# Roots of the input by groups in the first stage and another order of the last tiles, in a hybrid retention and attention step on one core

## The chip, the core and the metric

The kernel runs on one core of one Trainium2 chip. A core has five engines that run side by side, each through its own queue of instructions in order: PE (matrix products; its weight loads are listed apart as PEld), DVE (vectors), ACT (scalar functions and copies), POOL (GpSimd) and SP (here it only issues DMAs). Products are summed in PSUM banks; everything else lives in SBUF, which DMAs fill from the main memory. The metric is the device time of one execution in microseconds (us), the median of several runs.

## The reference, cut to what matters

The kernel computes one layer of a diffusion backbone for 128 context tokens and 512 latent tokens, all of width 1024, in float32. The change touches the two ends of the layer: the first modulated RMSNorm with what it feeds, and the last RMSNorm.

```python
def rms_scale(x):
    xf = x.astype(jnp.float32)
    return xf * lax.rsqrt(jnp.mean(xf * xf, axis=-1, keepdims=True) + EPS)

def adaln(cond, w_mod, b_mod):
    m = jax.nn.silu(cond) @ w_mod + b_mod
    return jnp.split(m[..., None, :], 6, axis=-1)

...
sh1, sc1, g1, sh2, sc2, g2 = adaln(c, w_mod[l], b_mod[l])
h = rmsnorm(xs, norm1_g[l]) * (1.0 + sc1) + sh1      # start: norm and modulation
y, _ = token_mixer(h, *mix_w, pos_lat, ctx)          # its first product is h @ w_in
...
xs = xs + g2 * conv_ffn(h, w_up[l], conv_w[l], conv_b[l], w_down[l])
y_sample = rmsnorm(xs, final_g)                      # end: last norm
```

## The kernel before

The 640 tokens are five tiles of 128: tile 0 is the context, tiles 1 to 4 the latent tokens. A float32 product is made of three products of rounded parts: each operand is split into a high part (a rounded copy) and a low part (the rest), and `mm3` (lines 158 to 161) multiplies high by high, high by low and low by high.

**The order of the work.** A planner of the programming layer gives each engine its order from the dependencies and its own estimate of times. Inside a `manual_schedule` block the engines that it names keep the order in which the program writes their instructions, and only work of other parts of the program may be put between. In the first stage (from line 406) these are PE, DVE and ACT; in the last (from line 1481) DVE and PE, so ACT, POOL and SP are ordered by the planner there. Every engine waits for the data of its next instruction and holds back what stands behind it.

**The first stage, lines 289 to 467.** SP issues all loads at the start, in a fixed order (lines 98 to 106 and 326 to 336): constants and small vectors, the five token tiles, and then by turns pieces of the adaLN weights `w_mod` (`mod_load`; five groups that serve 1, 1, 2, 2 and 2 of the eight column blocks k of the activations) and of the key and value weights (`kv_load`). The order of these loads is: mod 0, kv 0 and 1, mod 1, kv 2 and 3, mod 2, kv 4 to 7, mod 3, mod 4, the rest of the constants. None of them reuses a buffer.

- `x_square(t)` squares a token tile on ACT and sums it up, which takes an activation and the readout of its accumulator. `x_scale` takes the root of the sums by an integer estimate and three Newton steps on DVE (`rsqrt`, lines 202 to 220) for three tiles, later for two, and multiplies the tiles by it (line 349). `x_trans(t)` turns a tile over by eight PE transposes into two PSUM banks (line 356; there are five banks) and copies them out (line 358) to `xnT`, on ACT or DVE.
- `mod_mm(g)` (line 368) multiplies the condition by one group of `w_mod`, `mod_row` (line 376) copies the result out, and `mod_vec` (line 382) turns it into a vector by two small PE products, which DVE finishes (lines 384 and 386).
- `mod_hi(k)` scales and shifts block k on DVE (line 391) and makes its high part on ACT (line 393); `mod_lo(k)` makes the low part on DVE (line 396). `kv_hi` (line 319, ACT) and `kv_lo` (line 324, DVE) split the key and value weights in the same way, two blocks at a time.
- `z_kv(k)` multiplies block k of all five tiles by block k of these weights, 15 products of 512 columns into five banks that are summed over the eight blocks. Its argument `mid` puts a `mod_vec` between its second and third token tile.

The next stage's weights go through two buffers (`w_raw`, line 136, and `w_split`, lines 147 and 152), so their loads wait until `kv_lo` has read the old contents.

**The last stage, lines 1467 to 1513.** The last down-projection adds into `x1`. `last(t, c0, n)` makes the products of n columns of tile t, `down_add` multiplies them by the gate and adds them to `x1` on DVE (lines 1224 and 1225), and `square` sums the squares on ACT (line 1242) into `s7`. Tile 4 is done in one half of 512 and two quarters of 256 columns. `root_sum` adds up the sums on DVE, takes the power -0.5 on POOL (line 1252) and `root` makes one Newton step on DVE (lines 1260 to 1264), first for tiles 0 to 2 together, and then for tile 3 and tile 4. `gain` multiplies half a tile by the final gain `fg` (line 1270, on POOL or DVE), and `out` multiplies it by the root, on ACT (line 1277), or, where `fused`, by root and gain in one step on DVE (line 1275), and issues its DMA on SP (line 1279). There are ten such outputs of 256 KB.

Of the kernel before, what the change touches and what calls it, by code (L numbers as in the profile page):

```python
# [12 lines left out]
AF = mybir.ActivationFunctionType  # L13
ALU = mybir.AluOpType
# [4 lines left out]
P = 128  # L19
DM = 1024  # L20
KD = DM // P
NT = 5
# [4 lines left out]
NF = FF // P  # L27
EPS = 1e-6
O_Q, O_K, O_RQ, O_RK, O_RV, O_RG, O_GA, O_GR = 0, 1024, 1536, 2048, 2560, 3584, 4608, 5632
C_ID, C_SEL, C_SEL1, C_JV, C_RF, C_RB, C_MF, C_MB, C_IQ, C_NH, C_W = 0, 128, 136, 140, 142, 270, 398, 526, 654, 786, 787  # L30
HW = 322


# [36 lines left out]
def hybrid_step(ctx: ExitStack, tc: tile.TileContext, a: dict, o: dict):  # L70
# [131 lines left out]
    def rsqrt(pool, ss, n, inv_n, post=1.0):  # L202
        m = pool([P, n], tag=f"nm{n}", bufs=2)
        it = pool([P, n], I32, tag=f"ni{n}", bufs=2)
        y = pool([P, n], tag=f"ny{n}", bufs=2)
        tt = pool([P, n], tag=f"nt{n}", bufs=2)
        V.tensor_scalar(m, ss, inv_n, EPS, op0=ALU.mult, op1=ALU.add)
        V.tensor_scalar(it, m.bitcast(I32), 1, None, op0=ALU.logical_shift_right)
        V.tensor_scalar(y.bitcast(I32), it, -1, 0x5F3759DF, op0=ALU.mult, op1=ALU.add)
        V.tensor_scalar(m, m, -0.5, None, op0=ALU.mult)  # L210
        for _ in range(3):
            if n == 1:
                V.scalar_tensor_tensor(tt, y, m, y, op0=ALU.mult, op1=ALU.mult)
            else:
                V.tensor_mul(tt, y, y)
                V.tensor_mul(tt, tt, m)
            V.scalar_tensor_tensor(y, tt, 1.5, y, op0=ALU.add, op1=ALU.mult)  # L217
        if post != 1.0:
            V.tensor_scalar(y, y, post, None, op0=ALU.mult)  # L219
        return y  # L220
# [95 lines left out]
    def kv_hi(k0):  # L316
        h, kk = k0 // 4, k0 % 4
        wkv[k0] = [wraw[h][:, kk * 512:(kk + 2) * 512]] + [wp([P, 1024], F32R, tag="wh", bufs=8) for _ in range(2)]
        nc.scalar.copy(wkv[k0][1], wkv[k0][0])

    def kv_lo(k0, *part):
        raw, hi, lo = wkv[k0]
        s = slice(512 * part[0], 512 * part[0] + 512) if part else slice(0, 1024)
        V.tensor_sub(lo[:, s], raw[:, s], hi[:, s].bitcast(F32))
# [14 lines left out]
        sq = hflat[1][:, :DM]  # L339
        nc.scalar.activation(sq, xin[:, t, :], AF.Square, accum_out=ss[:, t:t + 1])  # L340

    def x_scale(t0, t1_, on_act=()):
        rs = rsqrt(t1, ss[:, t0:t1_], t1_ - t0, 1.0 / DM)
        for t in range(t0, t1_):
            r = rs[:, t - t0:t - t0 + 1]
            if t in on_act:
                nc.scalar.activation(xin[:, t, :], xin[:, t, :], AF.Copy, scale=r)
            else:
                V.tensor_scalar(xin[:, t, :], xin[:, t, :], r, None, op0=ALU.mult)  # L349

    def x_trans(t):
        for g in range(2):
            ps = mm([P, 512], tag="mm")
            for j in range(4):
                k = g * 4 + j
                nc.tensor.transpose(ps[:, j * P:(j + 1) * P], xin[:, t, k * P:(k + 1) * P], ident)  # L356
            copy = V.tensor_copy if g and t > 1 else nc.scalar.copy
            copy(xnT[g][:, :, t * P:(t + 1) * P], ps.rearrange("p (k t) -> p k t", k=4))

    mrow, psm = {}, {}  # L360

    def mod_mm(g, row=True):
        m = MG[g][1]
        psm[g] = aux([P, 512], tag="aux")
        for i in range(KD * m // 2):
            for j in range(4):
                k, cc = (i, j % 2) if m == 2 else (2 * i + j % 2, 0)
                nc.tensor.matmul(psm[g][32 * j:32 * j + 32, :P], s128[:, k, :],
                                 wmod[g][:, j // 2, k, cc * P:(cc + 1) * P],
                                 start=i == 0, stop=i == KD * m // 2 - 1)  # L370
        if row:
            mod_row(g)

    def mod_row(g):
        mrow[g] = t1([P, P], tag="mrow", bufs=2)
        V.tensor_copy(mrow[g], psm[g][:, :P])

    def mod_vec(g):
        k0, n = MG[g]
        sel = C_SEL if n == 2 else C_SEL1  # L380
        ps = aux([P, 512], tag="aux")
        nc.tensor.matmul(ps[:, :4 * n], mrow[g], cst[:, sel:sel + 4 * n], start=True, stop=True)
        m = mvec[:, :, k0:k0 + n, :]
        V.tensor_add(m, ps[:, :4 * n].rearrange("p (v j c) -> p v j c", v=2, j=n),
                     cv[:, 4:6, k0:k0 + n].unsqueeze(3).to_broadcast([P, 2, n, 2]))
        V.tensor_mul(m[:, 0], m[:, 0], cv[:, 2, k0:k0 + n].unsqueeze(2).to_broadcast([P, n, 2]))

    def mod_hi(k):
        xk = xnT[k // 4][:, k % 4]
        for c, s in ((0, slice(P, TOK)), (1, slice(0, P))):  # L390
            V.tensor_scalar(xk[:, s], xk[:, s], mvec[:, 0, k, c:c + 1],  # L391
                            mvec[:, 1, k, c:c + 1], op0=ALU.mult, op1=ALU.add)
        nc.scalar.copy(hT[0][:, k, :], xk)  # L393

    def mod_lo(k):
        V.tensor_sub(hT[1][:, k, :], xnT[k // 4][:, k % 4], hT[0][:, k, :].bitcast(F32))

    def z_kv(k, mid=None):
        wh, wl = (x[:, (k % 2) * 512:(k % 2) * 512 + 512] for x in wkv[k - k % 2][1:])
        for t in range(NT):  # L400
            ts = slice(t * P, (t + 1) * P)
            mm3(kvb[t], hT[0][:, k, ts], hT[1][:, k, ts], wh, wl, k == 0, k == KD - 1)
            if mid is not None and t == 1:
                mod_vec(mid)

    with tc.manual_schedule(engines={ET.PE, ET.DVE, ET.Activation}):
        ps = aux([P, 512], tag="aux")
        nc.tensor.transpose(ps[:, :80], crow, ident[:80, :80])
        s128 = cond_tile(t1)
        V.tensor_copy(cv.rearrange("p i k -> p (i k)"), ps[:, :80])  # L410
        th = t1([P, 2, 8], tag="th0")
        nc.scalar.activation(th, cv[:, 0:2, :], AF.Tanh, scale=0.5)
        V.tensor_scalar(cv[:, 4, :], cv[:, 4, :], 1.0, None, op0=ALU.add)
        V.scalar_tensor_tensor(th, th, 1.0, cv[:, 0:2, :], op0=ALU.add, op1=ALU.mult)
        V.tensor_scalar(s32, th.rearrange("p c k -> p k c"), 0.5, None, op0=ALU.mult)
        V.tensor_copy(s128[:, :, 0:2], s32)
        for t in range(NT):
            x_square(t)
        x_scale(0, 3)
        x_trans(0)  # L420
        x_trans(1)
        kv_hi(0)
        x_scale(3, 5)
        x_trans(2)
        x_trans(3)
        x_trans(4)
        mod_mm(0)
        mod_vec(0)
        mod_mm(1, False)
        mod_hi(0)  # L430
        kv_lo(0, 0)
        mod_lo(0)
        mod_row(1)
        mod_vec(1)
        mod_hi(1)
        kv_lo(0, 1)
        mod_lo(1)
        kvb = [mm([P, 512], tag="mm") for _ in range(NT)]
        z_kv(0)
        kv_hi(2)  # L440
        kv_lo(2)
        mod_mm(2)
        z_kv(1, 2)
        mod_hi(2)
        mod_hi(3)
        mod_lo(2)
        mod_lo(3)
        z_kv(2)
        kv_hi(4)
        kv_lo(4)  # L450
        mod_mm(3)
        z_kv(3, 3)
        mod_hi(4)
        mod_hi(5)
        mod_lo(4)
        mod_lo(5)
        kv_hi(6)
        kv_lo(6)
        mod_mm(4)
        z_kv(4, 4)  # L460
        mod_hi(6)
        mod_hi(7)
        mod_lo(6)
        mod_lo(7)
        z_kv(5)
        z_kv(6)
        z_kv(7)
# [800 lines left out]
    def gain(t, c0, eng):  # L1268
        x = x1[:, t, c0:c0 + 512]
        eng.tensor_mul(x, x, fg[:, c0:c0 + 512])  # L1270
# [210 lines left out]
    with tc.manual_schedule(engines={ET.DVE, ET.PE}):  # L1481
        def last(t, c0, n):
            last_mm(t, c0, n, (2, 3) if t < NT - 1 else (0, 1, 2, 3))
            down_add(bank[t, c0], t, c0)
            square(t, c0, n)

        for t in range(3):
            last(t, 0, 512)
            gain(t, 0, nc.gpsimd)
            last(t, 512, 512)  # L1490
        last(3, 0, 512)
        root_sum(0, 3)
        gain(3, 0, nc.gpsimd)
        last(3, 512, 512)
        root(0, 3)
        for u in range(3):
            out(u, 0)
        for u in range(2):
            out(u, 512, True)
        gain(3, 512, nc.gpsimd)  # L1500
        root_sum(3, 1)
        last(4, 0, 512)
        root(3, 1)
        out(2, 512, True)
        out(3, 0)
        out(3, 512)
        last(4, 512, 256)
        last(4, 768, 256)
        gain(4, 0, V)
        root_sum(4, 1)  # L1510
        root(4, 1)
        out(4, 0)
        out(4, 512, True)
    t7.close()
# [36 lines left out]
```

## Time and profile before

| what | value |
|---|---|
| three runs | 1188.34, 1190.0 and 1190.55 us, median 1190.0 |
| the profiled execution | 1187.15 us, of which the profile's span is 1185.4 us |
| granted clock of PE, mean | 0.996 |
| DMA bytes in the span | 139.02 MB |

The profile lists, in us from the start of its span, what each engine ran: start, duration, engine, line, operation, the tile written and the tiles read with their shapes, and in brackets how long the engine was idle before and what ended that time. "PEq" or "SPq" is an engine's sequencer. Merged rows end in the number of instructions. The chain of waits goes back from the last instruction, at each step to what released it. The waits view lists who waited for whom: total, number of times, longest. The windows view gives, for chosen stretches, the length and then the busy time and number of instructions of PE, PEld, DVE, ACT and POOL, PE's granted clock, the busy share of the 16 DMA engines and GB/s. The DMA view counts the packets of a stretch by size; one line of it gives a queue's packets, MB and the share of the DMA engines' time that its packets took.

### The profile page before, as it was taken

What the parts mean: (1) busy time and instruction counts of PE and PEld (TensorE: products, weight loads), DVE (VectorE), ACT (ScalarE), POOL (GpSimd) and SP (SyncE); (2) the same over time, 40 slices, a digit from 0 to 9 for tenths busy, and PEclk for the clock granted to TensorE, in tenths of its full rate; (3) what the DMA queues carried; (4) which work ended last, traced back from release to release, by engine and by line L of the source; (5) the groups of instructions that cost most, each with busy time, mean ns of one, the idle gap of its engine ahead of it and who ended that gap; (6) DMA issues with size and microseconds to landing.
All of it is one profiled execution on the core that took longest, in us unless ns stands there. A gap on an engine that the chain in (4) does not pass through costs nothing.

```text
span 1185.4 us, 18331 instructions
## 1 busy us (share of the span) xinstructions
PE 1152.0 (97%) x7317; PEld 1038.4 (88%) x7317; DVE 740.2 (62%) x1431; ACT 567.9 (48%) x1020; POOL 172.3 (15%) x174
## 2 busy tenths in 40 slices
PE   4999999999999999999999999999999999999995
PEld 3788899999988888888999988999989999899994
DVE  5676977663234436463333349959767688588887
ACT  4355656551132324443222235558557466565464
POOL 0032200000012100033011122011112111121013
PEclk9999999999999999999999999999999999999998
DMA  8922111115554431112122539445666667566552
GB/s 282 301 94 72 37 36 36 36 48 169 212 191 172 147 98 45 36 37 71 36 72 72 192 109 163 113 93 103 149 132 134 142 138 164 125 120 152 130 123 108
DMA packets 130917, 139.02 MB, mean 117 GB/s; under 512 B 26240, under 2 KB 98000, under 8 KB 130832
## 3 DMA queue, kind: packets, MB, share of 16 engines
q1 hardware_dynamic: 106592, 112.95, 29.5%
q0 software_dynamic: 24240, 24.91, 13.8%
q8 instruction: 57, 0.93, 0.3%
q14 instruction: 28, 0.23, 0.1%
HBM read 110.32 MB, written 6.03 MB: 98 GB/s over the span
## 4 chain that ended last, share of the span: by engine, by line
PE 90%; DVE 5%; issue 1%; ACT 1%; POOL 1%; DMA 0%; SPq 0%; POOLq 0%; ACTq 0%; DVEq 0%
DMA xin.u1.1_112<-in_x_sample 0%; POOL f0.s.5_3525 L902 0%; DVE acts.u2.2_101 L1066 0%; DVE x1.u1.1_6381 L1225 0%; DVE x1.u1.1_6381 L1038 0%; DVE acts.u1.1_100 L1065 0%; PE mm7.mm.9_7501 L1348 0%; PE mm7.mm.45_9655 L1345 0%; PE mm7.mm.33_8923 L1345 0%; PE mm7.mm.57_10407 L1345 0%; PE mm7.mm.21_8191 L1345 0%; PE mm7.mm.18_7942 L1345 0%; PE mm7.mm.30_8674 L1345 0%; PE mm7.mm.42_9406 L1348 0%; PE mm7.mm.42_9406 L1345 0%
## 5 line engine op out<-in xcount | busy, mean ns | idle before, releaser
L791 POOL TENSOR_TENSOR ret.r2k.6_3635<-ret.u5.5_3528,ret.u1.1_3521 128x256 f32<-128x256 f32 x2 | 1.4, 740 | 205.1 <-ACT ret.u5.5_3528 L787 205.1
L1359 DVE TENSOR_TENSOR t7.u4.4_6930<-t7.u4.4_6930,const.u1.1_70 128x322 f32<-128x322 f32 x10 | 5.0, 495 | 11.7 <-ACT const.u1.1_70 L1358 11.7
L840 DVE SCALAR_TENSOR_TENSOR ret2.u1.1_4322<-ret2.u1.1_4322,const.u14.14_94 64x128 f32<-64x128 f32 x24 | 6.8, 337 | 6.6 <-ACT ret2.u1.1_4322 L833 6.5
L152 DVE TENSOR_TENSOR weights.wh.183_6570<-weights.raw.181_6567,weights.wh.182_6569 128x1024 fp32r<-128x1024 f32 x1 | 1.2, 1224 | 14.3 <-ACT weights.wh.182_6569 L147 14.3
L356 PE MATMUL mm1.mm.1_180<-const.u1.1_70,xin.u1.1_112 128*128 128x128 f32 x4 | 1.1, 434 | 9.1 <-DVE xin.u1.1_112 L349 9.1
L525 POOL TENSOR_TENSOR p1.u1.1_618<-p1.u3.3_622,p1q.u1.1_612 128x512 f32<-128x512 f32 x1 | 1.6, 1588 | 57.0 <-DMA p1.u4.4_624<-in_cache_k 57.0
L842 DVE SCALAR_TENSOR_TENSOR ret2.u1.1_4322<-ret2.u1.1_4322,const.u14.14_94 64x128 f32<-64x128 f32 x24 | 6.6, 382 | 4.8 <-ACT ret2.u1.1_4322 L835 4.8
L1270 POOL TENSOR_TENSOR x1.u1.1_6381<-x1.u1.1_6381,weights.raw.410_10992 128x512 f32<-128x512 f32 x5 | 7.9, 1591 | 10.2 <-ACT x1.tm.112_11005 L1242 7.4
L793 DVE TENSOR_TENSOR ret.u5.5_3528<-ret.u5.5_3528,ret.u1.1_3521 128x512 f32<-128x512 f32 x5 | 3.5, 693 | 9.4 <-POOL ret.r2k.8_3706 L791 3.3
L793 DVE TENSOR_TENSOR ret.u4.4_3527<-ret.u4.4_3527,ret.u1.1_3521 128x512 f32<-128x512 f32 x5 | 3.5, 693 | 9.0 <-POOL ret.r2k.11_3886 L791 4.7
L356 PEld LDWEIGHTS mm1.mm.1_180<-const.u1.1_70,xin.u1.1_112 128*128 128x128 f32 x4 | 0.7, 216 | 9.3 <-DVE xin.u1.1_112 L349 9.3
L393 ACT CAST acts.u1.1_100<-f0.s.1_113 128x640 fp32r<-128x640 f32 x4 | 2.9, 728 | 11.2 <-DVE f0.s.1_113 L391 11.2
L152 DVE TENSOR_TENSOR weights.wh.108_4352<-weights.raw.106_4349,weights.wh.107_4351 128x1024 fp32r<-128x1024 f32 x1 | 1.2, 1225 | 10.3 <-ACT weights.wh.107_4351 L147 10.3
L147 ACT CAST weights.wh.112_4507<-weights.raw.111_4505 128x1024 fp32r<-128x1024 f32 x1 | 1.1, 1050 | 13.3 <-PE mm3.mm.36_4220 L160 13.3
L902 POOL TENSOR_TENSOR f0.s.5_3525<-f0.s.5_3525,ret2.ny20.11_4904 128x512 f32<-128x512 f32 x5 | 6.0, 1236 | 9.1 <-DVE ret2.ny20.11_4904 L219 9.1
L494 ACT ACTIVATE f0.s.3_724<-f0.s.3_724,p1q.ny20.11_892 128x128 f32<-128x128 f32 x20 | 6.0, 388 | 2.5 <-DVE p1q.ny20.11_892 L217 2.5
L393 ACT CAST acts.u1.1_100<-f0.s.2_114 128x640 fp32r<-128x640 f32 x4 | 2.9, 729 | 8.9 <-DVE f0.s.2_114 L391 8.9
L259 DVE COPY mod2.wr.9_4312<-aux3.aux.15_4279 128x128 f32<-128x128 f32 x1 | 0.3, 292 | 10.9 <-PE aux3.aux.15_4279 L256 10.9
L829 POOL DMA_DIRECT2D out_new_state_ret_fwd<-ret.r2k.25_4345 x1 | 0.7, 666 | 43.8 <-ACT ret.r2k.25_4345 L828 43.8
L1236 DVE TENSOR_TENSOR x1.u1.1_6381<-x1.u1.1_6381,gate.u1.1_5311 128x512 f32<-128x512 f32 x10 | 6.8, 685 | 0.0
L147 ACT CAST weights.wh.182_6569<-weights.raw.181_6567 128x1024 fp32r<-128x1024 f32 x1 | 1.1, 1055 | 11.5 <-PE mm3.mm.83_6401 L160 11.5
L147 ACT CAST weights.wh.67_3361<-weights.raw.66_3359 128x1024 fp32r<-128x1024 f32 x1 | 1.0, 1045 | 11.5 <-PE mm3.mm.8_3143 L195 11.5
(7024 smaller groups left out, 4878.6 us busy)
## 6 DMA issues: line engine op xcount, KB each, us to landing
spill.u1.1_6389<-x1.u1.1_6381 POOLq DMA_DIRECT2D x5, 512.0 KB, 5.0
xin.u1.1_112<-in_x_sample SPq DMA_DIRECT2D x4, 512.0 KB
p0.u5.5_130<-in_w_mod SPq DMA_DIRECT2D x2, 1024.0 KB
p0.u6.6_135<-in_w_mod SPq DMA_DIRECT2D x2, 1024.0 KB
p0.u7.7_138<-in_w_mod SPq DMA_DIRECT2D x2, 1024.0 KB
mod.wm.2_2921<-in_w_mod SPq DMA_DIRECT2D x1, 2048.0 KB
mod.wm.4_3072<-in_w_mod SPq DMA_DIRECT2D x1, 2048.0 KB
mod.wm.6_3227<-in_w_mod SPq DMA_DIRECT2D x1, 2048.0 KB
```

The source lines that it names most:

```text
L147: nc.scalar.copy(hi, rv)
L152: (lo_eng or V).tensor_sub(lo, rv, hi.bitcast(F32))
L356: nc.tensor.transpose(ps[:, j * P:(j + 1) * P], xin[:, t, k * P:(k + 1) * P], ident)
L393: nc.scalar.copy(hT[0][:, k, :], xk)
L494: nc.scalar.activation(x[:, j], x[:, j], AF.Copy, scale=rstd[:, j:j + 1])
L793: V.tensor_mul(z, z, r1[:, t, 0:1, :].to_broadcast([P, 8, 64]))
L840: V.scalar_tensor_tensor(Ss[0:64, hh, st + 1, j], Ss[0:64, hh, st, j], cdsel[0:64, h:h + 1], Ss[0:64, hh, st + 1, j], op0=ALU.mult, op1=AL ...
L842: V.scalar_tensor_tensor(Ss[64:128, hh, 2 - st, j], Ss[64:128, hh, 3 - st, j], cdsel[64:128, h:h + 1], Ss[64:128, hh, 2 - st, j], op0=ALU. ...
L902: nc.gpsimd.tensor_mul(ov, ov, rso[:, 4 * t:4 * t + 4].unsqueeze(2).to_broadcast([P, 4, P]))
L1236: V.tensor_mul(x1[:, t, gs], x1[:, t, gs], gb[:, t == 0, gs])
L1270: eng.tensor_mul(x, x, fg[:, c0:c0 + 512])
L1359: V.tensor_sub(u[1][:, hi_u], u[1][:, hi_u], u3[i])
```

## The change

Two places are edited, and one constant moves.

In the first stage the root is no longer taken by `rsqrt`. `x_sum` forms the mean of the squares on DVE, takes the power -0.5 on POOL, and prepares minus one half of the mean on DVE; `x_root` makes one Newton step on DVE. It is done for tiles 0 and 1, then 2 and 3, then 4. Scaling, transposes and the copies out of PSUM (`x_evac`) become steps of their own, in an order written out by hand: copies of tiles 0 and 1 and the first halves of the others go to ACT, the second halves of tiles 2 to 4 to DVE. The first `mod_row` stands behind the copies. The second `mod_vec` moves from in front of `z_kv(0)` into it (`z_kv(0, 1)`), and `mod_hi(1)`, `mod_lo(1)` and `kv_lo(0, 1)` come behind it. For the later pairs of blocks the order `hi, hi, lo, lo` becomes `hi, lo, hi, lo`. The constant -0.5 (`C_NH`) moves to column 142, into the first of the two loads of the constants, which takes 143 columns now.

In the last stage `last(4, 0, 512)` stands before the root of tiles 0 to 2, the quarters of tile 4 before `out(1, 0)`, and the fused outputs of tiles 0 to 2 behind them. The gain of tile 4's first half goes from DVE to POOL. The gain of tile 3's second half on POOL is gone; its output is a fused one on DVE, not one on ACT.

```diff
-C_ID, C_SEL, C_SEL1, C_JV, C_RF, C_RB, C_MF, C_MB, C_IQ, C_NH, C_W = 0, 128, 136, 140, 142, 270, 398, 526, 654, 786, 787
+C_ID, C_SEL, C_SEL1, C_JV, C_NH, C_RF, C_RB, C_MF, C_MB, C_IQ, C_W = 0, 128, 136, 140, 142, 143, 271, 399, 527, 655, 787
...
+    def x_sum(t0, n):
+        m, mh, y = (t1([P, n], tag=f"{g}{t0}") for g in ("xm", "xh", "xy"))
+        V.tensor_scalar(m, ss[:, t0:t0 + n], 1.0 / DM, EPS, op0=ALU.mult, op1=ALU.add)
+        nc.gpsimd.tensor_tensor(y, m, cst[:, C_NH:C_NH + 1].to_broadcast([P, n]), op=ALU.pow)
+        V.tensor_scalar(mh, m, -0.5, None, op0=ALU.mult)
+        xr[t0] = mh, y
+
+    def x_root(t0, n):
+        mh, y = xr[t0]
+        tt = t1([P, n], tag=f"xt{t0}")
+        if n == 1:
+            V.scalar_tensor_tensor(tt, y, mh, y, op0=ALU.mult, op1=ALU.mult)
+        else:
+            V.tensor_mul(tt, y, y)
+            V.tensor_mul(tt, tt, mh)
+        V.scalar_tensor_tensor(y, tt, 1.5, y, op0=ALU.add, op1=ALU.mult)
+        for t in range(t0, t0 + n):
+            xr[t] = mh, y, y[:, t - t0:t - t0 + 1]
...
+        A, D = nc.scalar.copy, V.tensor_copy
         for t in range(NT):
             x_square(t)
-        x_scale(0, 3)
+        x_sum(0, 2)
+        x_root(0, 2)
+        x_scale(0)
         x_trans(0)
+        x_scale(1)
         x_trans(1)
+        x_sum(2, 2)
+        x_evac(0, 0, A)
+        x_evac(0, 1, A)
+        x_root(2, 2)
+        x_scale(2)
+        x_sum(4, 1)
+        x_evac(1, 0, A)
+        x_trans(2)
+        x_scale(3)
+        x_root(4, 1)
+        x_scale(4)
+        x_evac(1, 1, A)
+        x_evac(2, 0, A)
+        x_trans(3)
+        x_evac(2, 1, D)
+        x_evac(3, 0, A)
         kv_hi(0)
-        x_scale(3, 5)
-        x_trans(2)
-        x_trans(3)
         x_trans(4)
-        mod_mm(0)
+        mod_mm(0, False)
+        x_evac(3, 1, D)
+        x_evac(4, 0, A)
+        x_evac(4, 1, D)
+        mod_row(0)
         mod_vec(0)
         mod_mm(1, False)
         mod_hi(0)
         kv_lo(0, 0)
         mod_lo(0)
         mod_row(1)
-        mod_vec(1)
+        kvb = [mm([P, 512], tag="mm") for _ in range(NT)]
+        z_kv(0, 1)
         mod_hi(1)
+        mod_lo(1)
         kv_lo(0, 1)
-        mod_lo(1)
-        kvb = [mm([P, 512], tag="mm") for _ in range(NT)]
-        z_kv(0)
         kv_hi(2)
         kv_lo(2)
         mod_mm(2)
         z_kv(1, 2)
         mod_hi(2)
+        mod_lo(2)
         mod_hi(3)
-        mod_lo(2)
         mod_lo(3)
...
         mod_mm(3)
         z_kv(3, 3)
         mod_hi(4)
+        mod_lo(4)
         mod_hi(5)
-        mod_lo(4)
         mod_lo(5)
         kv_hi(6)
         kv_lo(6)
         mod_mm(4)
         z_kv(4, 4)
         mod_hi(6)
+        mod_lo(6)
         mod_hi(7)
-        mod_lo(6)
         mod_lo(7)
...
         root_sum(0, 3)
         gain(3, 0, nc.gpsimd)
         last(3, 512, 512)
+        last(4, 0, 512)
         root(0, 3)
-        for u in range(3):
-            out(u, 0)
-        for u in range(2):
-            out(u, 512, True)
-        gain(3, 512, nc.gpsimd)
         root_sum(3, 1)
-        last(4, 0, 512)
-        root(3, 1)
-        out(2, 512, True)
-        out(3, 0)
-        out(3, 512)
+        out(0, 0)
         last(4, 512, 256)
         last(4, 768, 256)
-        gain(4, 0, V)
+        out(1, 0)
+        out(2, 0)
+        root(3, 1)
+        gain(4, 0, nc.gpsimd)
+        out(3, 0)
+        out(0, 512, True)
         root_sum(4, 1)
+        out(1, 512, True)
+        out(2, 512, True)
         root(4, 1)
+        out(3, 512, True)
         out(4, 0)
         out(4, 512, True)
```

More of the change, by code (lines that the diff above doesn't have):

```diff
@@ L340, in x_square, with x_scale, x_evac @@
         nc.scalar.activation(sq, xin[:, t, :], AF.Square, accum_out=ss[:, t:t + 1])
[L342 to L349, printed above, removed]
+    xr = {}
+    def x_sum(t0, n):
[15 more added lines that the diff above has]
+            xr[t] = mh, y, y[:, t - t0:t - t0 + 1]
+    def x_scale(t):
+        V.tensor_scalar(xin[:, t, :], xin[:, t, :], xr[t][2], None, op0=ALU.mult)
+    xps = {}
     def x_trans(t):
         for g in range(2):
-            ps = mm([P, 512], tag="mm")
+            xps[t, g] = mm([P, 512], tag="mm")
             for j in range(4):
                 k = g * 4 + j
-                nc.tensor.transpose(ps[:, j * P:(j + 1) * P], xin[:, t, k * P:(k + 1) * P], ident)
-            copy = V.tensor_copy if g and t > 1 else nc.scalar.copy
-            copy(xnT[g][:, :, t * P:(t + 1) * P], ps.rearrange("p (k t) -> p k t", k=4))
+                nc.tensor.transpose(xps[t, g][:, j * P:(j + 1) * P], xin[:, t, k * P:(k + 1) * P], ident)
+    def x_evac(t, g, copy):
+        copy(xnT[g][:, :, t * P:(t + 1) * P], xps[t, g].rearrange("p (k t) -> p k t", k=4))
     mrow, psm = {}, {}
```

## The prediction

> **What bounds the kernel now.** First the page: span, busy shares, the shares of the chain that ended last.
>
> ```profile
> span 1185.4 us, 18331 instructions
> ...
> PE 1152.0 (97%) x7317; PEld 1038.4 (88%) x7317; DVE 740.2 (62%) x1431; ACT 567.9 (48%) x1020; POOL 172.3 (15%) x174
> ...
> PE 90%; DVE 5%; issue 1%; ACT 1%; POOL 1%; DMA 0%; SPq 0%; POOLq 0%; ACTq 0%; DVEq 0%
> ```
>
> PE is the bound, except where the change works: at the start, before PE runs without a break, and at the end, when PE has finished. Next, PE's waits from 27 us to the end:
>
> ```profile
> PE aux1.aux.5_309 L382 <- DVE p0.mrow.19_307 L376: 2.2, 1, 2.2
> PE mm7.mm.12_7691 L1345 <- ACT t7.u1.1_6927 L1350: 1.3, 1, 1.3
> ```
>
> The first is the wait that ends at 26.93; behind it nothing longer than 1.3 us is left in 1146 us. So a microsecond that PE gains or loses in the first 50 us reaches the end almost whole, and the question is what PE gains there. The chain of waits of the start:
>
> ```profile
> 11.14 1.16 ACT acts.u2.2_101 L340 x2
> ...
> 14.69 0.76 DVE xin.u1.1_112 L349
> ...
> 15.50 1.11 PE mm1.mm.1_180 L356 x4
> 16.62 0.85 PE mm1.mm.2_186 L356 x4
> ...
> 19.12 0.44 PE mm1.mm.5_226 L356 x4
> ...
> 25.85 0.82 DVE acts.u2.2_101 L396
> ...
> 26.93 0.39 PE aux1.aux.5_309 L382 x2
> ...
> 30.91 1.88 PE aux1.aux.6_342 L368 x64
> ```
>
> The third square lets the root begin at 12.3, the root takes until 14.69, transposes start at 15.50 (four take 0.85, from 19.12 on 0.44), the first modulated slice is whole at 25.85 + 0.82 = 26.67, the second adaLN vector holds PE until 26.93, and at 30.9 comes the third adaLN product, mod_mm(2). This chain shows no transfer here, but the DMA view must be asked too. Its packet counts from 0 to 29.5 and from 0 to 30.5, its queue row from 0 to 46, and from the timeline the start of mod_mm(2):
>
> ```profile
> DMA packets 7955, 8.31 MB, mean 282 GB/s; under 512 B 303, under 2 KB 6642, under 8 KB 7954
> DMA packets 8148, 8.69 MB, mean 285 GB/s; under 512 B 304, under 2 KB 6656, under 8 KB 8147
> q1 hardware_dynamic: 12952, 14.19, 95.8%
> ...
> 30.83 1.95 PE L368 MATMUL aux1.aux.6_342<-p0.u5.5_130,p0.s128.8_146 128*32 128x128 f32 x64
> ```
>
> Packets under 2 KB are here w_mod's rows (512 B in the first two loads, 1 KB later), the small vectors and signals: 4096 + 2048 rows of the first three w_mod loads, 128 constant rows, 80 of bias and 304 shorter ones make exactly 6656. So the third load is still 14 packets short at 29.5 and whole by 30.5, in a queue that is 95.8% busy up to 46 us. mod_mm(2), which needs it, starts at 30.83. **Transfers stand at most 1.3 us behind the chain.**
>
> **The change part by part.** *Roots and transposes.* The second square is read out by 11.0, so the root of tiles 0 and 1 starts 1.28 us (one square) before today's 12.3. Its cost comes from the last stage's pow, of three columns and of one:
>
> ```profile
> 10.82 0.19 ACT L340 ACTIVATION_READ_ACCUMULATOR acts.u2.2_101<-xin.u1.1_112 128x1 f32 x1
> ...
> 1168.95 0.88 POOL L1252 TENSOR_TENSOR t7.ry.30_11078<-t7.rm.28_11076,const.u1.1_70 128x3 f32<-128x3 f32 x1 [0.90 <-DVE t7.rm.28_11076 L1251]
> 1174.80 0.54 POOL L1252 TENSOR_TENSOR t7.ry.34_11112<-t7.rm.32_11110,const.u1.1_70 128x1 f32<-128x1 f32 x1 [2.00 <-DVE t7.rm.32_11110 L1251]
> ```
>
> Two columns lie between 0.54 and 0.88; I take 0.71. With one small step before (0.2), two handovers (0.1) and three behind (0.6) that is 1.6 us against 14.69 - 12.3 = 2.4. The first scaling moves to 12.6, the transposes to 13.4: 2.1 us earlier. DVE waits for POOL at each of three roots; behind the waiting step on DVE stand only scalings that need the root, or a later one. POOL has nothing else before 57 us. The copies, split between ACT and DVE, and mod_mm(0) follow 2.0 us earlier.
>
> *mod_vec(1) into z_kv(0).* PE no longer waits for it: the first slice is whole at 26.67 - 2.0 = 24.7, z_kv(0) runs from there; today it lasts from 27.3 (26.93 + 0.39) to 30.8, 3.5 us; two of its products (0.5) need no low part and come before 24.7, the vector (0.3) is now inside, so it ends at 24.7 + 3.5 - 0.5 + 0.3 = 28.0, 2.8 us earlier. Then PE stands before mod_mm(2), whose load is whole between 29.5 and 30.5 and whose signal is out by 30.83. No transfer of this stage waits for a computed value, and the change moves none of these DMAs, so the load comes when it came: gain between 1.3 and 0. I take 30.7, **-0.1**, the row nearest to the start seen. The 2.8 us are spent waiting for data. The moved kv_lo(0,1) and the copies that change engines I cost at nothing: all are done before 30.7, where PE waits; without that cover kv_lo(0,1) alone, half of a 1.2 us step, would be 0.6. The constant that moves into the first load adds one column to 142, nothing that a chain of 512 KB loads shows.
>
> *Pairs hi, lo, hi, lo.* Where today two scalings, two casts and two subtractions overlap, DVE now waits for the cast in each pair. Today's second slice (one pair) and the slices 4 and 5 with what stands behind them, on DVE, ACT and PE:
>
> ```profile
> 27.75 0.81 DVE L391 TENSOR_SCALAR f0.s.1_113<-f0.s.1_113,p0.u1.1_111 128x512 f32<-128x512 f32 x2
> 29.35 0.83 DVE L396 TENSOR_TENSOR acts.u2.2_101<-f0.s.1_113,acts.u1.1_100 128x640 fp32r<-128x640 f32 x1 [0.20 <-ACT acts.u1.1_100 L393]
> ...
> 42.68 0.29 DVE L376 COPY p0.mrow.21_456<-aux1.aux.8_423 128x128 f32<-128x128 f32 x1 [3.24 <-PE aux1.aux.8_423 L368]
> ...
> 44.76 1.52 DVE L391 TENSOR_SCALAR f0.s.2_114<-f0.s.2_114,p0.u1.1_111 128x512 f32<-128x512 f32 x4
> 46.36 1.56 DVE L396 TENSOR_TENSOR acts.u2.2_101<-f0.s.2_114,acts.u1.1_100 128x640 fp32r<-128x640 f32 x2
> 48.03 1.23 DVE L324 TENSOR_TENSOR weights.wh.10_486<-weights.raw.2_133,weights.wh.9_485 128x1024 fp32r<-128x1024 f32 x1
> 49.17 0.28 DVE L376 COPY p0.mrow.22_522<-aux1.aux.10_489 128x128 f32<-128x128 f32 x1
> ...
> 45.60 1.44 ACT L393 CAST acts.u1.1_100<-f0.s.2_114 128x640 fp32r<-128x640 f32 x2 [7.42 <-DVE f0.s.2_114 L391]
> 46.94 1.05 ACT L319 CAST weights.wh.9_485<-weights.raw.2_133 128x1024 fp32r<-128x1024 f32 x1
> ...
> 49.83 0.28 PE L382 MATMUL aux1.aux.11_530<-const.u1.1_70,p0.mrow.22_522 128*128 128x8 f32 x2
> ```
>
> From scaling to subtraction is 29.35 - 27.75 = 1.60, the cast of 0.72 between them. Slice 4: scaling at 44.76, subtraction at 46.36. Slice 5: scaling at 47.1 (the subtraction holds DVE for 0.75; today it begins at 45.5), cast from 47.95, subtraction at 48.7. On ACT kv_hi(6) stands behind that second cast: today 46.94, then 48.6, and through at 49.65 (1.05). So kv_lo(6) starts at 49.66 instead of 48.03, mod_row(4) behind it at 50.8, and PE, which stands at mod_vec(4) by 49.83, gets its row at 51.1: **+1.3**. At slices 2 and 3 the same delay is covered, for mod_row(3) waits 3.24 us for PE today; uncovered it would be 1.6, which is also my upper bound here. The lower is nothing, if the planner's other work shifts.
>
> *Last stage.* PE's last product of tile 4's first half, POOL's gains against DVE, and the end:
>
> ```profile
> 1170.16 0.40 PE L161 MATMUL acc7.acc.55_11117<-weights.wh.406_10982,gt.gt1.28_10933 128*128 128x512 f32 x1
> ...
> 1169.81 2.98 POOL L1270 TENSOR_TENSOR x1.u1.1_6381<-x1.u1.1_6381,weights.raw.410_10992 128x512 f32<-128x512 f32 x2
> 1170.31 1.26 DVE L1262 TENSOR_TENSOR t7.rt.31_11095<-t7.ry.30_11078 128x3 f32<-128x3 f32 x1
> ...
> 1180.89 0.75 DVE L1275 SCALAR_TENSOR_TENSOR x1.u1.1_6381<-x1.u1.1_6381,t7.ry.38_11183,weights.raw.410_10992 128x512 f32<-128x512 f32 x1
> ...
> 1181.64 0.81 SPq L1279 DMA_DIRECT2D out_y_sample<-x1.u1.1_6381  x2
> ```
>
> A product of three columns lasts 1.26 us, until POOL's first gain (half of 2.98) is over; the next one waits for the second gain in the same way. The change takes the second gain away and puts the last tile's addition in front of the root. Tile 4's first half is ready at 1170.56, its two steps (0.7 each) end at 1172.05, the root of 0 to 2 is ready at 1172.6, and after root_sum(3) the quarters follow from 1173.05, of 0.9 us each. Now gain(4,0) runs on POOL, 1.5 us from about 1173.55, behind the pow of tile 3, and the first quarter's addition starts at about 1173.5: whichever comes first holds the other. With DVE first, the second quarter's addition waits until 1175.1 and ends at 1175.5; with POOL first, at 1176.3. Behind it come root(3) (0.4), root_sum(4) (0.5), root(4) (0.4), four fused outputs of 0.75 that overlap by 0.05 to 0.1, and the handovers: the last output ends at 1180.2 or 1180.9 instead of 1181.64. Queued behind DVE's waits are only these. The extra fused output of tile 3 stands where the gain of 0.7 that goes to POOL stood. Gain 1.4 or 0.7; I take **-1.1**, the middle, since the two starts lie within 0.05 us; the far end is no gain (rival B). The outputs' ten DMAs stay ten, in another order on SP's queue.
>
> The Trainium skill (GPSIMD Engine Reference, Key points) says that GpSimd shares its SBUF interfaces with VectorE and contends with instructions that have two SBUF inputs. By that rule a fused output, which reads two tensors, would also wait for a gain that comes late, up to 1.5 us, and the stage would gain nothing; in the order above the gain is over before the first of them.
>
> *Sum:* -0.1 + 1.3 - 1.1 = +0.1 us. The profiled execution took 1187.15 us with 1185.4 of span, so 1187.25 for it; the median of the runs shown is 1190.0, so **1190.1 us**.
>
> **Rivals.** *A: PE's clock drops while it waits* (slower). The windows view, with the granted clock after POOL's column:
>
> ```profile
> 1172.60:1173.40 0.80, 0.79 (x7) 0.58 (x5) 0.73 (x3) 0.29 (x1) 0.20 (x1) 1.00 0.00 0
> 1173.40:1176.04 2.64, 0.00 (x0) 0.00 (x0) 2.54 (x7) 1.66 (x3) 0.54 (x1) 1.00 0.52 194
> 1176.04:1179.00 2.96, 0.00 (x0) 0.00 (x0) 2.86 (x9) 2.44 (x7) 0.00 (x0) 0.50 1.01 381
> ```
>
> PE's last product ends at 1173.4 and at 1176.04 the clock is 0.50: 2.64 us of idleness were enough once. The new wait (28.0 to 30.7) is 2.7 us; today's of 2.2 us was not followed by slow products. At the start the slow transposes lasted from 15.50 to 18.9, 3.4 us of work at half speed, which is 1.7 us lost; with a second such stretch 3.4. Taken at 2.55: 1190.1 + 2.55 = 1192.65. It decides from an idle time of some 2.6 us on. The Trainium skill (TensorE: Matmul & The Clock Gate, HAM oscillation) sets the limit at idle gaps over about 3.4 us, counted in free-running windows. By that rule a gap of 2.7 us would cost nothing, and the sum stays; the end of this trace, 2.64 us, speaks against a limit that long.
>
> *B: the outputs bunch up* (no gain at the end). Output rows and the transfer rate in 40 slices of 0.325 us from 1173 to 1186:
>
> ```profile
> 1173.83 0.83 SPq L1279 DMA_DIRECT2D out_y_prompt<-x1.u1.1_6381  x2
> ...
> GB/s 0 0 0 0 0 302 365 378 397 385 391 347 397 397 378 366 378 391 384 384 372 397 44 0 0 0 0 0 0 321 384 366 397 145 0 0 0 0 0 0
> ```
>
> Eight outputs fill 17 slices: 0.69 us each, and the last leaves 2.3 us after DVE's end (1184.0). If ACT takes the quarters' squares ahead of out(1,0), that one is ready at 1176.8 (addition 1175.5, square 0.6, scaling 0.65), its data flow 0.85 later, as the first did today (1173.83, data in slice 5), and nine outputs end at 1177.7 + 9 x 0.69 = 1183.9: no gain, 1191.2. Against it: both halves of tile 0 left first, though the program has tiles 1 and 2 between them, so the planner orders by readiness.
>
> *C: transfers come at the early bound and the row is not late* (-1.3, 0, -1.1): 1187.6 to 1189, centre 1188.5.
>
> *D: the change does what it says:* 2.8 us at the start and 1.4 at the end, 1185.8. Against it, the packet counts.
>
> **How the numbers follow.** Forecast 0.42, A 0.20, B 0.13, C 0.16, D 0.09. A measurement of this kernel can tell about 0.2% (2.4 us) from no change: below 1187.6 is faster, above 1192.4 slower. Faster: D and a half of C, 0.17. Slower: A's upper part and A with B, 0.17. Same: 0.66. The range leaves out D's far end and A's: 1187.0 to 1193.0; the forecast's own is 1188.8 to 1191.6 (load 1.2 early, or the end without gain and the row at 1.6).
>
> **What would show it.** Right: first transposes near 13.4; z_kv(0) ending near 28; PE then waiting over 2 us for w_mod, mod_mm(2) again at 30.7; a PE wait of about 1.3 us on mod_row(4) near 50; DVE's last output 0.7 to 1.4 us nearer to PE's end. Wrong: mod_mm(2) before 29.5, which would need the third load earlier; mod_vec(4) without a wait; products of double length after 30 us (A); a gap in the outputs between tile 0 and tile 1 (B).

## The result and the profile after

| | before | after |
|---|---|---|
| median, us (20 runs each) | 1189.8 (1186.62 to 1190.55) | 1191.58 (1189.18 to 1193.85) |
| the profiled execution, us | 1187.15 | 1192.46 |
| its span, us | 1185.4 | 1190.7 |

The ratio after to before is 1.0016, 95% interval 1.0009 to 1.0023: 0.16% slower, or 1.8 us. The two profiled executions lie further apart, 5.3 us. That this is not the same number turns out to be part of the answer.

The page of the kernel after: span, engines, and the chain that ended last.

```profile
span 1190.7 us, 18327 instructions
...
PE 1156.5 (97%) x7317; PEld 1041.0 (87%) x7317; DVE 737.5 (62%) x1419; ACT 567.4 (48%) x1019; POOL 174.7 (15%) x177
...
PE 89%; DVE 5%; SPq 1%; ACT 1%; DMA 1%; issue 1%; POOL 1%; DVEq 0%; POOLq 0%; ACTq 0%
```

PE runs the same 7317 products but is busy 4.5 us longer: some ran slower. Its waits from 27 us to the end:

```profile
PE mm1.mm.16_720 L159 <- DVE p1.vt.7_627 L552: 2.9, 1, 2.9
PE aux1.aux.6_337 L386 <- DMA p0.u5.5_130<-in_w_mod: 2.3, 1, 2.3
PE mm7.mm.12_7686 L1383 <- ACT t7.u1.1_6922 L1388: 1.3, 1, 1.3
PE aux1.aux.11_525 L400 <- DVE p0.mrow.26_517 L394: 1.1, 1, 1.1
```

Before had a wait of 2.2 us at the second adaLN vector and the one of 1.3 us. Now there are three others: 2.3 us for the third `w_mod` load (forecast), 1.1 us for a late `mod_row(4)` (forecast), and 2.9 us on DVE's copy of a key/value bank (not forecast). PE's timeline shows the first of them:

```profile
13.27 1.11 PE L373 MATMUL mm1.mm.1_171<-const.u1.1_70,xin.u1.1_112 128*128 128x128 f32 x4 [7.13 <-DVE xin.u1.1_112 L364]
...
27.86 0.41 PE L386 MATMUL aux1.aux.6_337<-p0.u5.5_130,p0.s128.8_146 128*32 128x128 f32 x4
30.57 3.53 PE L386 MATMUL aux1.aux.6_337<-p0.u5.5_130,p0.s128.8_146 128*32 128x128 f32 x60 [2.30 <-DMA p0.u5.5_130<-in_w_mod]
```

Transposes begin 2.2 us earlier than before and `z_kv(0)` is through by 27.86. Four products of `mod_mm(2)` find their rows there, and the other 60 stand until 30.57. They then take 3.53 us, where 64 took 1.95 before. The DMA view says why they stood (0 to 29.5 and 0 to 30.5):

```profile
DMA packets 7959, 8.32 MB, mean 282 GB/s; under 512 B 303, under 2 KB 6645, under 8 KB 7958
DMA packets 8155, 8.70 MB, mean 285 GB/s; under 512 B 304, under 2 KB 6656, under 8 KB 8154
```

The row of 30.5 is within seven packets of that of the kernel before (8148), with the same 6656 under 2 KB: the transfers did not move. Why the products were slow, the windows view shows; ahead of each stretch at half clock stands one in which PE was mostly idle.

```profile
27.04:30.45 3.41, 1.23 (x8) 0.52 (x6) 2.56 (x3) 1.63 (x2) 0.00 (x0) 1.00 1.07 365
30.45:33.86 3.41, 3.29 (x60) 2.93 (x60) 0.00 (x0) 0.00 (x0) 0.00 (x0) 0.50 1.07 360
...
64.59:68.00 3.41, 0.81 (x4) 0.33 (x2) 3.17 (x12) 0.42 (x2) 1.75 (x5) 1.00 0.00 0
68.00:71.41 3.41, 3.10 (x7) 2.48 (x8) 3.41 (x14) 2.82 (x8) 0.93 (x1) 0.50 0.13 41
```

The wait of 2.9 us is read from DVE's timeline, here of the kernel after:

```profile
60.49 1.28 DVE L581 TENSOR_SCALAR const.u17.17_97<-const.u16.16_96 128x16 f32<-128x16 f32 x1
...
63.49 1.22 DVE L588 TENSOR_SCALAR const.u16.16_96<-const.u16.16_96 128x16 f32<-128x16 f32 x1
64.75 0.39 DVE L587 TENSOR_TENSOR const.u16.16_96<-const.u16.16_96,const.u18.18_98 128x16 f32<-128x16 f32 x1
...
66.61 0.17 DVE L588 TENSOR_SCALAR const.u16.16_96<-const.u16.16_96 128x16 f32<-128x16 f32 x1
...
67.42 0.42 DVE L549 TENSOR_TENSOR kv.u4.4_603<-mm1.mm.11_304,kv.u3.3_602 128x256 fp32r<-128x256 f32 x1
67.75 0.41 DVE L552 COPY p1.vt.7_627<-mm1.mm.11_304 128x256 f32<-128x256 f32 x1
```

and of the kernel before:

```profile
60.64 0.42 DVE L511 TENSOR_TENSOR kv.u4.4_608<-mm1.mm.11_318,kv.u3.3_607 128x256 fp32r<-128x256 f32 x1 [1.32 <-PE mm1.mm.12_319 L161]
60.98 0.42 DVE L514 COPY p1.vt.7_632<-mm1.mm.11_318 128x256 f32<-128x256 f32 x1
...
63.86 0.16 DVE L540 TENSOR_SCALAR const.u16.16_96<-const.u11.11_91 128x16 f32<-128x16 f32 x1
```

`const.u16` to `const.u18` are the temporaries of the decay constants (`decay_consts`), a chain of small steps that belongs to a later part of the kernel. Before, the planner put it behind the first copies of the key/value banks; after, it put the body of the chain ahead of them, and PE, which needs a bank back for its next products, waits until 68.31. The edit names neither. The new place also lies beside POOL's products of the following stage (60.31 to 66.33): there eleven steps of the chain, from 60.49 on, took 5.5 us together, and the same eleven took 2.0 us in the kernel before, behind those products. So the order and POOL together make this wait; no run parts the two. SP's timeline shows the same decision: their load is issued at 39.91, and was issued at 56.25 (first row after, second before).

```profile
39.91 1.36 SPq L773 DMA_DIRECT2D const.u11.11_91<-in_decay_fwd  x1
```

```profile
56.25 0.51 SPq L735 DMA_DIRECT2D const.u11.11_91<-in_decay_fwd  x1
```

The end, from the timelines of DVE, PE and POOL of the kernel after, in order of time:

```profile
1179.30 0.15 DVE L1300 TENSOR_TENSOR t7.rt.31_11108<-t7.ry.30_11073 128x3 f32<-128x3 f32 x1
...
1180.41 0.28 PE L161 MATMUL acc7.acc.57_11139<-weights.wh.408_10982,gt.gt1.28_10928 128*128 128x256 f32 x1
...
1180.65 0.43 DVE L1263 TENSOR_TENSOR x1.u1.1_6376<-x1.u1.1_6376,x1.tm.129_11134 128x256 f32<-128x256 f32 x1
1180.70 1.50 POOL L1308 TENSOR_TENSOR x1.u1.1_6376<-x1.u1.1_6376,weights.raw.410_10987 128x512 f32<-128x512 f32 x1
...
1181.45 1.04 DVE L1263 TENSOR_TENSOR x1.u1.1_6376<-x1.u1.1_6376,x1.tm.131_11152 128x256 f32<-128x256 f32 x1
...
1182.73 0.74 DVE L1313 SCALAR_TENSOR_TENSOR x1.u1.1_6376<-x1.u1.1_6376,t7.ry.30_11073,weights.raw.410_10987 128x512 f32<-128x512 f32 x1
...
1186.14 0.75 DVE L1313 SCALAR_TENSOR_TENSOR x1.u1.1_6376<-x1.u1.1_6376,t7.ry.38_11171,weights.raw.410_10987 128x512 f32<-128x512 f32 x1
```

PE ends at 1180.69 and DVE at 1186.89, 6.2 us later; before it was 1181.64 - 1173.39 = 8.25. The root's product of three columns takes 0.15 instead of 1.26 us, since no gain runs beside it. POOL's gain now holds the addition of the second quarter instead (1.04).

**The account of the profiled executions**, from the start of the same product in both traces (after minus before):

| where | the two starts, us | difference | what came in |
|---|---|---|---|
| first transposes | 13.27, 15.50 | -2.2 | earlier roots |
| `mod_mm(2)` goes on | 30.57 (60 left), 30.83 (64 left) | -0.4 | load wait takes the lead away |
| `mod_mm(2)` ends | | +1.3 | half clock: 60 products 3.53 instead of 1.83 us, +1.7 |
| `mod_vec(4)` | 52.42, 49.83 | +2.6 | `mod_row(4)` late, +1.3 |
| first product after the banks | 68.31, 62.53 | +5.8 | decay chain ahead of the bank copies, +3.2 |
| PE's end | 1180.69, 1173.39 | +7.3 | second half clock, 68.00 to 71.41, +1.6, less 0.1 over the rest |
| end of span | 1190.7, 1185.4 | +5.3 | last stage, -2.0 |

### The profile page after: what moved, and what is told of

Its sections match the earlier page's. It is cut to its first block, busy times and chain, and to the rows that moved or that the text cites. A ratio compares the mean times of both kernels' runs of the same rounds, so it can differ in the third digit from the quotient of the medians.

```text
span 1190.7 us, 18327 instructions
## 1 busy us (share of the span) xinstructions
PE 1156.5 (97%) x7317; PEld 1041.0 (87%) x7317; DVE 737.5 (62%) x1419; ACT 567.4 (48%) x1019; POOL 174.7 (15%) x177
## 4 chain that ended last, share of the span: by engine, by line
PE 89%; DVE 5%; SPq 1%; ACT 1%; DMA 1%; issue 1%; POOL 1%; DVEq 0%; POOLq 0%; ACTq 0%
DMA p0.u5.5_130<-in_w_mod 1%; SPq L313 0%; SPq L307 0%; POOL f0.s.5_3520 L940 0%; DVE acts.u2.2_101 L1104 0%; PE aux1.aux.6_337 L386 0%; DVE x1.u1.1_6376 L1076 0%; DVE acts.u1.1_100 L1103 0%; PE mm1.mm.16_720 L159 0%; PE mm7.mm.45_9650 L1383 0%; PE mm7.mm.9_7496 L1386 0%; PE mm7.mm.57_10402 L1383 0%; PE mm7.mm.33_8918 L1383 0%; PE mm7.mm.63_10768 L1385 0%; PE mm7.mm.54_10133 L1383 0%
```

## The experiments

Theory: those terms, and beside them that most executions of the kernel before lose PE's clock in their own wait of 2.2 us, which the profiled one did not. In the first four, the kernel before took 1189.48 us beside them (21 runs), in the last four 1189.56 (15 runs).

**e1: the first stage of after, the last stage of before.** The order of the last stage is undone, in short:

```diff
-        last(4, 0, 512)
         root(0, 3)
...
+        last(4, 0, 512)
...
-        gain(4, 0, nc.gpsimd)
+        gain(4, 0, V)
```

> The first stage of the changed kernel with the last stage of the kernel before. Theory (the first stage costs, the last stage gains about 2.0 us): some 3.8 us slower than before, 1193 to 1194. Rival (the last stage is what costs): within 0.5 us of before.

Measured: 1192.92 us (1192.59 to 1194.51), ratio 1.0031 (1.0020 to 1.0043). PE's waits:

```profile
PE mm1.mm.16_720 L159 <- DVE p1.vt.7_627 L552: 2.9, 1, 2.9
PE aux1.aux.6_337 L386 <- DMA p0.u5.5_130<-in_w_mod: 1.6, 1, 1.6
...
PE aux1.aux.11_525 L400 <- DVE p0.mrow.26_517 L394: 1.1, 1, 1.1
```

All three waits come with the first stage, and the loss of 3.4 us with them, just under the 3.8 of the theory. In this execution only the second half clock came (66.38 to 69.80).

**e2: the first stage of before, the last stage of after.** In short, as a change of the kernel after:

```diff
-        x_sum(0, 2)
-        x_root(0, 2)
-        x_scale(0)
+        x_scale(0, 3)
...
-        z_kv(0, 1)
+        z_kv(0)
...
-        mod_lo(2)
         mod_hi(3)
+        mod_lo(2)
```

> The first stage of the kernel before with the last stage of the changed one. Theory: 2.0 us faster than before, 1187.3 to 1188.3, and from PE's last product to the end of the span 10.0 us instead of 12.0. Rival (the last stage is what costs): 1190 to 1192.

Measured: 1187.39 us (1184.95 to 1188.47), ratio 0.9985 (0.9976 to 0.9994): the last stage alone gains 2.1 us; +3.4 and -2.1 make +1.3, beside 1.8 measured for both. From PE's last product to the end of the span it is 10.0 us, as the theory said. PE ends at 1176.11 in this profile, 2.7 us later than in that of before, though the first stage is the same. Its windows:

```profile
22.64:26.05 3.41, 1.51 (x38) 1.11 (x34) 2.37 (x7) 0.72 (x1) 0.00 (x0) 1.00 1.10 350
26.05:32.88 6.83, 6.10 (x15) 4.89 (x16) 4.46 (x9) 1.67 (x2) 0.00 (x0) 0.50 1.08 364
```

Two windows at half clock behind the old wait of 2.2 us cost those 2.7 us: `mod_mm(2)` starts at 33.47, in the profile of before at 30.83. The profiled execution of before had no such stretch, although its wait was as long. In each trace the changes of the clock lie a whole number of windows of 3.41 us apart (in the kernel after at 30.45, 33.86, 68.00 and 71.41), and by that grid the wait of before, from 24.7 to 26.9, lies across the boundary of two windows:

```profile
22.33:25.75 3.42, 1.97 (x58) 1.41 (x46) 2.31 (x7) 0.65 (x1) 0.00 (x0) 1.00 1.09 353
25.75:29.16 3.41, 2.23 (x11) 1.88 (x12) 2.75 (x7) 0.64 (x2) 0.00 (x0) 1.00 1.09 354
```

PE is busy in them for 1.97 and 2.23 us, and for 1.51 us in the window of e2 above.

**e3: after, with the old order of the pairs** (three times):

```diff
         mod_hi(2)
-        mod_lo(2)
         mod_hi(3)
+        mod_lo(2)
         mod_lo(3)
```

> The changed kernel with the old order hi, hi, lo, lo of the later pairs. Theory: the wait of PE for the fifth adaLN row (1.1 us near 51) is gone, and because DVE is through earlier the planner puts the decay constants behind the copies of the key and value banks again, so the wait near 65 (2.9 us) is gone too: 1186.5 to 1188.5. Rival (the order of the pairs is harmless, only the clock and the load count): 1191 to 1192.

Measured: 1186.24 us (1184.81 to 1186.45), ratio 0.9970 (0.9959 to 0.9982), 5.3 us under the kernel after and 0.3 under the theory's range. The wait for the third load is still there, the other two are gone, and SP issues the decay load late again:

```profile
PE aux1.aux.6_337 L386 <- DMA p0.u5.5_130<-in_w_mod: 2.5, 1, 2.5
```

```profile
57.62 0.51 SPq L773 DMA_DIRECT2D const.u11.11_91<-in_decay_fwd  x1
```

So both the wait at `mod_vec(4)` and the planner's new place for the decay chain hang on the order of the pairs. PE's end, 1174.70, is 1.3 us behind before's: the -0.4 and +1.7 of the account.

**e4: after, with the decay loads held back.** One small copy behind the bank copies writes into their buffer, so that the load of the forward decay must wait for it; the load that follows overwrites it.

```diff
     for t in range(NT):
         evac_kv(t, kvb[t])
+    V.tensor_copy(dec[:, 0, :], vv[0][:, NT - 1, :8].bitcast(F32))
```

> The changed kernel, but the decay constants can be loaded only after the last key and value bank is copied out; one DVE copy of 128x8 is added for it. Theory: PE's wait near 65 falls from 2.9 us to under 0.5, the second drop of the clock goes with it, the wait near 51 stays at 1.1: 1187 to 1189. Rival (that wait has another cause, such as the weights that arrive late): the wait stays over 2 us and the time at 1191 to 1192.

Measured: 1186.36 us (1185.98 to 1187.69), ratio 0.9976 (0.9966 to 0.9985), 5.2 us under the kernel after and 0.6 under the theory's range. PE's waits:

```profile
PE aux1.aux.11_525 L400 <- DVE p0.mrow.26_517 L394: 1.1, 1, 1.1
PE aux1.aux.6_337 L386 <- DMA p0.u5.5_130<-in_w_mod: 1.0, 1, 1.0
```

The wait of 2.9 us is gone and with it the second half clock, while the wait of 1.1 us stays: the two are separate, and the decay chain was the larger one. PE ends 0.4 us before e3's although it kept that wait: in this execution the half clock fell on 24.01 to 27.43, and not on `mod_mm(2)`. There it slowed `z_kv(0)`, and the wait for the load behind it was shorter by that (1.0 instead of 2.3 us).

**e5: before, with PE kept busy in its wait of 2.2 us.** `busy(9)` is nine products of 512 columns, whose result nothing uses.

```diff
         mod_row(1)
+        busy(9)
         mod_vec(1)
```

> The kernel before, with nine more products of 512 columns (result unused) put on PE between the second adaLN product and mod_vec(1), where PE stands idle for 2.2 us; nine take 9 x 0.23 = 2.1 us at full clock. Theory (most executions of the kernel before lose PE's clock for about two windows of 3.41 us near 26 us, because PE idles in its first stage; the profiled execution that the prediction was reckoned from did not): no drop near 26 us, and a median of 1186.5 to 1187.7, some 2 to 3 us under the kernel before at 1189.5. Rival (the difference of 2.7 us between profile and median has another cause, and the new products at best take the idle time): 1189 to 1190, unchanged.

Measured: 1187.45 us (1186.49 to 1188.02), ratio 0.9983 (0.9974 to 0.9992). Work that does nothing makes the kernel 2.1 us faster. PE's timeline (the added products, then `mod_vec(1)`):

```profile
24.32 2.34 PE L401 MATMUL aux1.aux.5_309<-weights.wh.3_204 128*128 128x512 f32 x9
26.61 0.39 PE L382 MATMUL aux1.aux.6_319<-const.u1.1_70,p0.mrow.19_307 128*128 128x4 f32 x2
```

`mod_vec(1)` is hardly earlier than before (26.93), and the clock stays at 1.00 in this profile from 18.30 on. The median comes to 0.3 us from the 1187.15 of before's profiled execution: that one was a before without a clock drop, and the typical before has one.

**e6: e3, with the third `w_mod` load ahead of blocks 2 and 3 of the key and value weights** (one load of 0.52 MB, called block 2 in the expectation).

```diff
-    kv_load(2, 2)
     mod_load(2)
+    kv_load(2, 2)
```

> The kernel after, with the old order hi, hi, lo, lo of the pairs (as in e3) and with the third load of w_mod one step earlier, ahead of the key and value weights of block 2, which are 0.52 MB. Theory (mod_mm(2) waits for the third load alone, in a queue that is full): 0.52 MB at 0.35 MB per us are 1.5 us, mod_mm(2) starts near 29.1 instead of 30.6, its wait falls from 2.5 us to about 1, and the time from e3's 1186.2 to 1184 to 1185.3, if block 2's weights, late by as much, do not hold PE in their turn. Rival (the load is not what PE waits for, or the weights behind it are then late by the same): 1186.2, unchanged.

Measured: 1184.28 us (1184.15 to 1184.67), ratio 0.9960 (0.9946 to 0.9975): the theory's number, and 2.0 us under e3. PE's timeline has no wait ahead of `mod_mm(2)`:

```profile
29.39 2.04 PE L386 MATMUL aux1.aux.6_337<-p0.u5.5_129,p0.s128.8_146 128*32 128x128 f32 x64
```

The transfer order, not the chain of roots, held this product. In this execution a half clock from 24.11 to 27.52 slowed `z_kv(0)`, so the profile cannot tell how long PE would have waited without it; the five times, 1184.15 to 1184.67 us at mean granted clocks of 0.995 to 0.998, show no cost of it. The rival was right in a small part: ACT waits 1.85 us for the weights that now come behind that load and begins `kv_hi(2)` at 30.79 (27.59 in e3), `kv_lo(2)` and `mod_row(2)` on DVE follow late, and PE stands 0.33 us at `mod_vec(2)`.

**e7: e3 with `busy(9)` ahead of `mod_mm(2)`** (result unused).

```diff
+        busy(9)
         mod_mm(2)
```

> The kernel of e3 (after, with the old order of the pairs), with nine more products of 512 columns (result unused) ahead of mod_mm(2), where PE idles for 2.5 us; they take about 2.1 us at full clock, and mod_mm(2) still starts near 30.6. Theory (the idle time lets the clock drop for a window of 3.41 us near 30.5, which costs 1.3 to 1.7 us beside the wait itself): no drop near 30.5, 1184.6 to 1185.3. Rival (the idle time costs only itself): 1186.2, unchanged.

Measured: 1185.33 us (1185.14 to 1185.47), ratio 0.9969 (0.9956 to 0.9981), 0.9 us under e3. The timeline:

```profile
29.05 2.20 PE L419 MATMUL aux1.aux.6_337<-weights.wh.3_241,acts.u1.1_100 128*128 128x512 f32 x9
31.18 1.96 PE L386 MATMUL aux1.aux.7_347<-p0.u5.5_130,p0.s128.8_146 128*32 128x128 f32 x64
```

`mod_mm(2)` starts later than in e3 (30.73) but lasts 1.96 us, not 3.46 for 60 products: the half clock cost more than the 0.5 us that the fillers overran.

**e8: e6 with four such products ahead of `mod_mm(2)`.**

```diff
+        busy(4)
         mod_mm(2)
```

> The kernel of e6 (old pairs, third load of w_mod earlier), with four more products of 512 columns (result unused, 0.9 us) ahead of mod_mm(2). Theory: what is left of the wait is filled, no drop of the clock near 30 us, 1183.5 to 1184.7, the fastest of all. Rival (the wait of e6 is too short to drop the clock, so the products add nothing or delay mod_mm(2)): as e6 or up to 0.5 us above it.

Measured: 1184.31 us (1184.19 to 1184.72), ratio 0.9961 (0.9948 to 0.9973), the same as e6: the rival. Where the wait is gone, the fillers have nothing to protect; they push `mod_mm(2)` from 29.39 to 29.98. So e6 needs no dummy work and is, with e8, the fastest version: 5.3 us under before by its own comparison, some 7.3 under after.

## Why the prediction was right, and where it was not

The forecast was 1190.1 us and no change; 1191.58 and +0.16% came. **The sum was right by cancellation**: several of its steps hold; the size of the last stage, the clock and the order of the work behind 50 us do not. That they nearly balance is luck.

- *Roots and transposes earlier by 2.1 us:* -2.2. `z_kv(0)` was to end at 28.0 and ended at 27.86.
- *The load takes that gain away, -0.1 (bounds -1.3 and 0):* -0.4. The packet counts were the right view, and e6 confirms it from the other side: move the load and the gain appears.
- *Pairs hi, lo, hi, lo, +1.3:* +1.3, with `mod_row(4)` late behind `kv_lo(6)` as described; e3 takes it away.
- *Last stage, -1.1:* mis-sized, -2.0 in the profile and -2.1 in e2. The race went as the better branch (-1.4) had it: the first quarter's addition (1180.65) began just ahead of POOL's gain (1180.70), and the second quarter's addition then took 1.04 us beside it. The gain was over (1182.20) before the first fused output (1182.73). Of the other 0.6 us, half was there when that addition ended: 1182.49, where the prediction's 1175.5 and the 7.3 us of PE's end give 1182.8. From there to DVE's last output the prediction had 4.7 us and it took 4.4. The 4.7 holds two errors that offset each other: it counts four fused outputs behind the addition, where the program has five, and leaves some 0.6 us for handovers. The first fused output starts before `root_sum(4)`, whose power on POOL then runs beside further outputs; all five with both small steps take 4.16 us, from 1182.73 to 1186.89.
- *Rival A, the clock:* it was no rival but part of the course. It dropped behind the wait of 2.3 us and cost 1.7 us, the price that the rival gave one stretch. Its point of decision, "an idle time of some 2.6 us on", was wrong: 2.2 us were enough in e2. The prediction had ruled the old wait harmless from one execution.
- *B* did not happen: the span ends 3.8 us behind DVE's last output in both kernels. *C* and *D* fell with the load.
- **The step that failed** is the first one: that "a microsecond that PE gains or loses in the first 50 us reaches the end almost whole". It took the order behind 50 us for fixed. The prediction named "the planner's other work" only as a reason for a lower bound. The planner put the decay chain ahead of the bank copies: +3.2 us, and +1.6 by the clock behind that wait. e3 and e4, in two ways, take both back. So the term of the pairs, +1.3 with an upper bound of 1.6, was the price of the late row alone; taking the new order back in e3 was worth 5.3 us.

Why the median moved by 1.8 us and not by 5.3: the profile of before was a run without a clock drop before PE's end, 2.65 us under its median, while the typical run of before has one (e2's profile, e5's time). The times say the same: of the 36 executions of before beside the experiments four took 1186.45 to 1186.83 us at a mean granted clock of 0.996, and the others 1188.2 to 1190.89, all but one at 0.993 to 0.995. The profile of after, with two drops, lies 0.9 us over its own median, so 5.3 - 2.65 - 0.9 gives the 1.8. Without any clock term the account is 5.3 - 1.7 - 1.6 = +2.0, and the two fastest runs of after took 1189.2 us, 2.0 over the profiled execution of before. The prediction added its change to the median and did not ask what the 2.65 us were; that the clock takes about as much from both medians is luck. So is the place of 1191.58: ten of the 20 runs took 1192.08 us or more, the other ten 1191.08 or less, and the median is the middle of that gap.

Open: by what estimate the planner moves the decay chain when the pairs are reordered. The runs show that it does, not why.

## What to carry to other kernels

An edit inside a hand-written order can move work that a planner places around it: after each such edit compare the order of every engine's later work, not the edited stretch alone. Before speeding up a chain, count the packets of the next load; if it lands with the chain, move the load first. Where PE must wait 2 us or more, price a stretch at half clock as well, and do not take one profiled execution for the typical one.

## What the runs showed of the hardware

- PE's clock went to half for stretches of 3.41 us or twice that. Windows of 3.41 us with 0.81, 1.23 and 1.51 us of PE busy were followed by half clock, though the waits in them were 2.9, 2.3 and 2.2 us. The Trainium skill (TensorE: Matmul & The Clock Gate, HAM oscillation) sets the rule at idle gaps over about 3.4 us; the window's length agrees, the limit on the gap does not. The length of the wait alone does not decide: the same wait of 2.2 us in the profile of before, spread over two windows with 1.97 and 2.23 us of PE busy, was not followed by half clock. Nor is there a sharp limit on the busy time: a window with 1.86 us was not followed by half clock in e1 (28.83 to 32.25), and one with 2.24 us was followed by it in e4 (20.60 to 24.01) and not in the kernel after (20.21 to 23.63).
- DVE steps of 128x16, which took 0.17 us alone, took 1.2 us or 0.38 us while POOL multiplied (1.28 at 60.49, 0.39 at 64.75, 0.17 at 66.61). Steps with one tensor input were held too (L581, L588), not only those with two.
